# A transformer block with experts on one core: sums of squares on TensorE, lower parts on GpSimd, attention scores a step later

## The chip, the core and the metric

The kernel runs on one core of a Trainium2 chip. The metric is device time in microseconds. Five engines run their own instruction streams, each in the order in which the program wrote them: TensorE (PE), VectorE (DVE), ScalarE (ACT), GpSimd (POOL) and SyncE (SP), which here only issues transfers.

## The reference

One block on 256 tokens and 256 context tokens of width 2048, in fp32. The parts that the change touches:

```python
mod = silu(c) @ ada_w + ada_b              # the same for the context
h   = rmsnorm(x, norm1_g) * (1 + sc1) + sh1    # and hc for the context
# differential attention, 8 heads, keys from context and tokens
s = einsum(q, k) * scale; p = softmax(s); a = p[0] - lam * p[1]
# gated linear attention, 4 heads, in both directions
q_in, k_in, k_st = q * exp(b), k * exp(-b), k * exp(b_last - b)
att = tril(q_in @ k_in.T)
# experts: top 16 of 128 * 128 for each of 8 heads
act = gelu(einsum("pd,ped->pe", h, u[idx])); out = einsum("pe,ped->pd", act * g, v[idx])
```

`rmsnorm(x, g)` is `x * rsqrt(mean(x * x) + eps) * g`.

## The kernel before

Every weight matrix comes through a `Stream` (line 37) in blocks of 128x1024 fp32, 512 KB each. SP loads a block; ScalarE rounds it to a high part (L90); VectorE or GpSimd subtracts to get the low part (L92); TensorE multiplies both. A stream has a few raw buffers, whose next load waits until the parts have been made. Blocks named in `whole` are not split: TensorE takes them as plain fp32 (L339). Which engine makes the low part, `share` says.

Work beside the products is written as generators in `Jobs` lanes: after each step of a product loop `tick` resumes each lane's first job, and a `yield n` puts the next piece n ticks further. Since every engine keeps the written order, the place of a `yield` fixes where the instructions stand between the matmuls.

**First stage** (lines 219 to 358). 64 blocks of the modulation weights, in eight column groups of eight blocks, go through stream `A`; in the last three groups (5, 6 and 7 of 0 to 7) TensorE also makes products of the stage that follows (`pre`, L214 to L216), which need H, the normalized and modulated x, in a high and a low part. `norm_job` loads x, squares it on ScalarE (L295), adds the squares on GpSimd (L296), sums them over the partitions with one matmul (L298), takes the reciprocal root on ScalarE with a Newton step on VectorE (L181 to L183), and multiplies x by it on GpSimd (L303). `cols_job` turns a group's results into columns (L255, L259), and from the second group on every other group starts an `h_job`, which scales and shifts four of x's 16 slices (VectorE, L275), rounds them (ScalarE, L278) and subtracts (VectorE, L281).

**Attention** (`da_head`, L436 and after). Keys and queries `tq` are normalized and rotated on VectorE (last operation L453), `scores(0)` multiplies them (L465), then come maxima, exponentials, the combination of the two softmaxes, and the transposes `turn` (L491). A head's steps run beside product loops of 12 matmuls to a step (L413 to L416).

**Linear attention** (`gla_head`). VectorE makes `q_in`, `k_in` (L640) and `k_st` (L643), TensorE multiplies the first two (`inner`, L653) and transposes the third (`turn`, L667).

**Experts.** After the query products the stream `W` goes on with 256 blocks of `u` and 256 of `v` (L1222, L1223 for `u`), while VectorE finds each token's experts (routing, L1037 and after). `W.share` at L1154 gives three of four lower parts to GpSimd from there on.

Of the kernel before, what the change touches and what calls it, by code (L numbers as in the profile page):

```python
# [7 lines left out]
F32 = mybir.dt.float32  # L8
# [3 lines left out]
AF = mybir.ActivationFunctionType  # L12
OP = mybir.AluOpType
# [6 lines left out]
KT = 16  # L20
EPS = 1e-6
FMAX = 3.0e38
NGA = 8
NPRE = 3
# [111 lines left out]
def block_kernel(ctx, tc, a, out):  # L136
    nc = tc.nc
    ctx.enter_context(tc.manual_schedule())
    V, S, G, PE = nc.vector, nc.scalar, nc.gpsimd, nc.tensor
# [23 lines left out]
    W = Stream(nc, wpool, blocks, 3, 3, 2, on_pool)  # L163
# [7 lines left out]
    eps = cst.tile([128, 1], F32)  # L171
# [3 lines left out]
    def rsqrt(pool, v, shape, name, ytag=None, ttag=None):  # L175

        y = pool.tile(shape, F32, name=name + "y", tag=ytag or name + "y", bufs=1)
        t = pool.tile(shape, F32, name=name + "t", tag=ttag or name + "t", bufs=1)
        S.activation(t, v, AF.Ln, bias=eps[:, 0:1])
        S.activation(y, t, AF.Exp, scale=-0.5)  # L180
        V.scalar_tensor_tensor(t, v, EPS, y, op0=OP.add, op1=OP.mult)  # L181
        V.scalar_tensor_tensor(t, t, -0.5, y, op0=OP.mult, op1=OP.mult)
        V.scalar_tensor_tensor(y, t, 1.5, y, op0=OP.add, op1=OP.mult)  # L183
        return y
# [34 lines left out]
    with ExitStack() as st:  # L219
        p0 = st.enter_context(tc.tile_pool(name="p0", bufs=1))  # L220
        some = {i for i in range(64) if i % 8 in (2, 5)}
        late = set(range(8 * (8 - NPRE), 64))
        crow = p0.tile([16, 128], F32, name="crow", tag="sq", bufs=2)
        nc.scalar.dma_start(crow, a["c_row"])
        A = Stream(nc, p0, [a["ada1"][i] for i in range(64)], 5, 4, 3, some & late, some - late)
        A.load_to(5)
        nc.sync.dma_start(P, a["params"])
        nc.sync.dma_start(K0, a["consts0"])
        gs1 = p0.tile([128, KT, 2], F32)
# [17 lines left out]
        ss = sp("ss")  # L247
        acols = sp("acols")[:, 0:64].rearrange("p (a b) -> p a b", b=2)
        rows, normed = {}, [0]
        tot = p0.tile([128, 512], F32)  # L250

        def cols_job(g):
            r = rows.pop(g)
# [12 lines left out]
                jobs.add("h", h_job(k0), 1)  # L266

        def h_job(k0):
            while normed[0] < k0 + 4:
                yield 1  # L270
            for n in range(6):
                if n < 4:
                    k = k0 + n
                    for s, c0 in ((1, 0), (0, 256)):
                        V.tensor_scalar(xs[:, k, c0:c0 + 256], xs[:, k, c0:c0 + 256], gs1[:, k, s:s + 1],  # L275
                                        ada1[:, k, s:s + 1], op0=OP.mult, op1=OP.add)
                if 1 <= n < 5:
                    S.activation(H[:, 0, k0 + n - 1], xs[:, k0 + n - 1], AF.Copy)  # L278
                if n >= 2:
                    k = k0 + n - 2  # L280
                    V.tensor_tensor(H[:, 1, k], xs[:, k], H[:, 0, k].bitcast(F32), OP.subtract)  # L281
                yield 1

        def norm_job():
            for k in range(0, KT, 4):
                nc.sync.dma_start(xs[:, k:k + 4, 0:256], a["ctx_t"][:, k:k + 4])
                nc.sync.dma_start(xs[:, k:k + 4, 256:512], a["x_t"][:, k:k + 4])
                yield 1
            yield 2
            for k in range(KT):  # L290
                if k == 0:
                    S.activation(tot, xs[:, 0], AF.Square)
                else:
                    sq = p0.tile([128, 512], F32, name="sq", bufs=2)
                    S.activation(sq, xs[:, k], AF.Square)  # L295
                    G.tensor_tensor(tot, tot, sq, OP.add)  # L296
                yield 1
            PE.matmul(ss, o2048, tot, start=True, stop=True)  # L298
            yield 1
            rstd = rsqrt(p0, ss, [128, 512], "n1")  # L300
            yield 2
            for k in range(0, KT, 2):
                G.tensor_tensor(xs[:, k:k + 2], xs[:, k:k + 2],  # L303
                                rstd[:, None, :].to_broadcast([128, 2, 512]), OP.mult)
                normed[0] = k + 2
                yield 1

        def lam_job():
            lamv = p0.tile([128, 4, 64], F32, name="lamv", tag="sq", bufs=2)
# [116 lines left out]
    def da_head(pool, j, tq, sq, sk, vals):  # L426
# [24 lines left out]
        yield 1  # L451
        V.tensor_tensor(xq, xq, K[:, C_COS:C_COS + 256][:, None, :].to_broadcast([128, 2, 256]), OP.mult)
        V.tensor_tensor(xq, xq, sw, OP.add)  # L453
        yield 2
        mx = pool.tile([128, 4], F32, name="mx", bufs=2)
        z = pool.tile([128, 4], F32, name="z", bufs=2)
        r = pool.tile([128, 4], F32, name="r", bufs=2)
# [135 lines left out]
    def gla_head(pool, h, kt, qt, vn, gr):  # L593
# [43 lines left out]
        def state_exp(d):  # L637
            S.activation(ks[d], ks[d], AF.Exp, scale=1.0 / 16)
            V.tensor_tensor(qi[d], qi[d], qt, OP.mult)
            V.tensor_tensor(ki[d], ki[d], kt[:, 256:512], OP.mult)  # L640
# [7 lines left out]
        def inner(d):  # L648
            if d == 0:
                att[0] = sp("att").rearrange("p (d b i) -> p d b i", d=2, b=2)  # L650
            for b in range(2):
                c = slice(b * 128, (b + 1) * 128)
                PE.matmul(att[0][:, d, b], ki[d][:, c], qi[d][:, c], start=True, stop=True)  # L653
# [62 lines left out]
        state_exp(0)  # L716
        yield 1
        decays(1)
        inner(0)
        yield 1  # L720
        state_in(0)
        state_exp(1)
        yield 1
        turn(0)
        inner(1)
        yield 1
        turn_copy(0)
        state_in(1)
        inner_mask()
        yield 1  # L730
        turn(1)
        state_mm(0, 0)
        yield 1
        turn_copy(1)
        state_up(0, 0, 2)
# [192 lines left out]
    with tc.tile_pool(name="xpool", bufs=1) as pool:  # L928
# [7 lines left out]
        sq = {}  # L936
# [214 lines left out]
        if h == 1:  # L1151
            jobs.add("score", rows())
    nwq[0] = W.i
    W.share = lambda s: s % 4 != 0  # L1154
    W.flush()
    jobs.limit("score", 0)
    jobs.add("route", weigh())
# [323 lines left out]
```

## Time and profile before

| what | value |
|---|---|
| median of three runs | 2553.24 us (2549.06 to 2555.9) |
| the profiled execution | 2551.56 us beside a span of 2549.8 |
| TensorE matmuls busy | 2427.0 us, 95% |
| VectorE busy | 1950.9 us, 77% |
| ScalarE busy | 1298.1 us, 51% |
| GpSimd busy | 690.7 us, 27% |
| bytes moved | 678.86 MB, mean 266 GB/s |

Times are in microseconds from the start of the span. Matmuls are pipelined, so the distance between two starts is what one costs in a row; the duration that a row gives is longer. A busy share over the span is an average over stages with different limits.

### The profile page before, as it was taken

The page shows a single profiled execution, that of the slowest core. Times are in us where ns is not written, and L with a number is a line of the kernel's source. Part 1 is how long each engine was busy: PE and PEld are TensorE (multiplying, and loading weights), DVE is VectorE, ACT ScalarE, POOL GpSimd, SP SyncE. Part 2 cuts the span into 40 slices and gives each one's busy share as a digit, 9 for nine tenths or more (in the row PEclk, how much of TensorE's full clock was granted, in tenths as well). Part 3 has the DMA queues.
Part 4 walks back from the last instruction along what each step waited for, and adds up shares of the span by engine and source line. Part 5 has one row for each costly group of instructions (what it writes and reads, how often), then busy time and mean ns, then how long its engine had stood idle before and what let it go on. Part 6 is the DMA issues. An engine that isn't in the chain of part 4 may idle for free.

```text
span 2549.8 us, 39628 instructions
## 1 busy us (share of the span) xinstructions
PE 2427.0 (95%) x15236; PEld 2188.9 (86%) x15236; DVE 1950.9 (77%) x2584; ACT 1298.1 (51%) x1947; POOL 690.7 (27%) x343
## 2 busy tenths in 40 slices
PE   6799999999999999989899999999999999999999
PEld 3477888888899999989898999999998888888887
DVE  4868888657864656457997888889986888888866
ACT  5453444333444444453355999955554444444443
POOL 4441111222201334037487121211120232223100
PEclk8799999999999999999899999999999999999999
DMA  8665555456646776657476899999997999999985
GB/s 299 227 215 185 182 198 173 140 176 247 223 133 206 252 260 217 221 158 236 140 229 217 326 326 325 328 367 393 394 386 263 368 378 384 362 375 380 350 254 159
DMA packets 196494, 678.86 MB, mean 266 GB/s; under 512 B 21840, under 2 KB 54192, under 8 KB 179152
## 3 DMA queue, kind: packets, MB, share of 16 engines
q1 hardware_dynamic: 155456, 521.36, 59.1%
q0 software_dynamic: 19008, 137.44, 13.9%
q10 hardware_dynamic: 21840, 17.53, 2.3%
q8 instruction: 119, 1.95, 0.3%
q14 instruction: 71, 0.58, 0.1%
HBM read 660.83 MB, written 11.68 MB: 264 GB/s over the span
## 4 chain that ended last, share of the span: by engine, by line
PE 66%; DVE 16%; DMA 7%; issue 2%; ACT 2%; ACTq 0%; SPq 0%; POOL 0%; DVEq 0%; POOLq 0%
PE acc L1222 10%; PE acc L214 6%; PE acc L216 6%; PE acc L215 6%; PE yb L1364 5%; PE acc L1223 5%; PE yb L1363 5%; PE ya L1366 4%; PE ya L1367 4%; PE ya L1365 4%; DMA back<-park 4%; DVE wlo L92 2%; PE acc L413 2%; PE acc L415 2%; PE acc L416 2%
## 5 line engine op out<-in xcount | busy, mean ns | idle before, releaser
L92 DVE TENSOR_TENSOR wlo<-wraw,whi 128x1024 fp32r<-128x1024 f32 x669 | 841.2, 1278 | 283.9 <-ACT whi L90 280.0
L90 ACT ACTIVATE whi<-wraw 128x1024 fp32r<-128x1024 f32 x824 | 853.2, 1053 | 277.9 <-PE ya L1366 53.8
L92 POOL TENSOR_TENSOR wlo<-wraw,whi 128x1024 fp32r<-128x1024 f32 x155 | 400.7, 2594 | 786.3 <-ACT whi L90 768.3
L1222 PE MATMUL acc<-H,whi 128*128 128x384 f32 x2048 | 612.0, 364 | 0.0
L1223 PE MATMUL acc<-H,wlo 128*128 128x192 f32 x2048 | 521.6, 255 | 21.3 <-DVE wlo L92 20.9
L1223 PEld LDWEIGHTS acc<-H,wlo 128*128 128x128 f32 x2048 | 394.7, 193 | 27.9 <-DVE wlo L92 27.6
L1222 PEld LDWEIGHTS acc<-H,whi 128*128 128x128 f32 x2048 | 388.7, 190 | 0.0
L214 PE MATMUL acc<-H,whi 128*128 128x256 f32 (+1 forms) x1248 | 377.2, 302 | 1.4 <-ACT whi L90 1.4
L216 PE MATMUL acc<-H,wlo 128*128 128x256 f32 (+1 forms) x1248 | 371.7, 298 | 1.0 <-DVE wlo L92 0.8
L215 PE MATMUL acc<-H,whi 128*128 128x256 f32 (+1 forms) x1248 | 371.3, 298 | 0.0
L214 PEld LDWEIGHTS acc<-H,whi 128*128 128x128 f32 x1248 | 239.2, 192 | 20.3 <-issue 12.1
L216 PEld LDWEIGHTS acc<-H,wlo 128*128 128x128 f32 x1248 | 239.1, 192 | 8.4 <-DVE wlo L92 1.2
L215 PEld LDWEIGHTS acc<-H,whi 128*128 128x128 f32 x1248 | 239.3, 192 | 5.8
L1166 POOL DMA_INDIRECT gat<-v_rows,sidx x64 | 121.0, 1890 | 368.7 <-DVE ys L1188 307.1
L389 DVE SCALAR_TENSOR_TENSOR a<-a,cb 128x1024 f32<-128x1024 f32 x128 | 194.1, 1520 | 23.4 <-DMA a<-ada 23.3
L1363 PE MATMUL yb<-whi,as 128*128 128x512 f32 x512 | 204.2, 399 | 2.6 <-DVE as L191 2.6
L1166 POOL DMA_INDIRECT gat<-u_rows,sidx x64 | 94.3, 1474 | 409.4 <-DVE gat L1173 409.0
L1364 PE MATMUL yb<-wlo,as 128*128 128x512 f32 x512 | 203.9, 398 | 0.4 <-DVE wlo L92 0.4
L1366 PE MATMUL ya<-whi,as 128*128 128x512 f32 x512 | 203.1, 397 | 0.0
L1367 PE MATMUL ya<-wlo,as 128*128 128x512 f32 x512 | 202.7, 396 | 0.0
L1365 PE MATMUL ya<-whi,as 128*128 128x512 f32 x512 | 202.6, 396 | 0.0
L1188 DVE SCALAR_TENSOR_TENSOR ys<-gat,sg,ys 128x2048 f32<-128x2048 f32 x63 | 147.9, 2348 | 24.7 <-DMA gat<-v_rows,sidx 24.7
(327 smaller groups left out, 4156.4 us busy)
## 6 DMA issues: line engine op xcount, KB each, us to landing
wraw<-u SPq DMA_DIRECT2D x256, 512.0 KB
wraw<-v_rows SPq DMA_DIRECT2D x256, 512.0 KB
wraw<-w_a SPq DMA_DIRECT2D x162, 512.0 KB
a<-ada SPq DMA_DIRECT2D x128, 512.0 KB
wraw<-ada SPq DMA_DIRECT2D x64, 512.0 KB
wraw<-w_br SPq DMA_DIRECT2D x32, 512.0 KB
wraw<-w_o SPq DMA_DIRECT2D x32, 512.0 KB
wraw<-w_q SPq DMA_DIRECT2D x32, 512.0 KB
```

Of the source, the lines that this page charges most:

```text
L90: nc.scalar.activation(hi, r, AF.Copy)
L92: e.tensor_tensor(lo, r, hi.bitcast(F32), OP.subtract)
L214: PE.matmul(acc[:, :n], hi[:, c], mh, start=(k == 0), stop=False)
L215: PE.matmul(acc[:, :n], hi[:, c], ml, start=False, stop=False)
L216: PE.matmul(acc[:, :n], lo[:, c], mh, start=False, stop=(k == nk - 1))
L1222: PE.matmul(acc[:, 0:2 * TD], hi[:, c], H2[:, k], start=(k == 0), stop=(k == KT - 1), skip_group_check=True)
L1223: PE.matmul(acc[:, 0:TD], lo[:, c], H2[:, k, 0:TD], start=False, stop=(k == KT - 1), skip_group_check=True)
L1363: PE.matmul(yb[n], hb, hi[:, c], start=first, stop=False)
L1364: PE.matmul(yb[n], hb, lo[:, c], start=False, stop=last)
L1365: PE.matmul(ya[n], h0, hi[:, c], start=first, stop=False)
L1366: PE.matmul(ya[n], h1, hi[:, c], start=False, stop=False)
L1367: PE.matmul(ya[n], h0, lo[:, c], start=False, stop=last)
```

## The change

In the first stage the stream gets six raw buffers instead of five and other blocks for GpSimd and for the unsplit way (in both versions VectorE makes 48 of the 64 lower parts; GpSimd made 6 and makes 10; 10 blocks were unsplit and 6 are). `norm_job` sums the squares with 16 matmuls into one PSUM bank and no longer multiplies x; `h_job` does that, with operations that take two tensors and a scalar. The scores in `da_head` are written one tick later, the two `inner` calls and the mask in `gla_head` one step later. `W.share` gives GpSimd all lower parts of the first twelve expert blocks.

```diff
--- before.py
+++ after.py
@@ -219,11 +219,10 @@
     with ExitStack() as st:
         p0 = st.enter_context(tc.tile_pool(name="p0", bufs=1))
         some = {i for i in range(64) if i % 8 in (2, 5)}
-        late = set(range(8 * (8 - NPRE), 64))
         crow = p0.tile([16, 128], F32, name="crow", tag="sq", bufs=2)
         nc.scalar.dma_start(crow, a["c_row"])
-        A = Stream(nc, p0, [a["ada1"][i] for i in range(64)], 5, 4, 3, some & late, some - late)
-        A.load_to(5)
+        A = Stream(nc, p0, [a["ada1"][i] for i in range(64)], 6, 4, 3, some, {2, 13, 26, 37, 50, 61})
+        A.load_to(6)
         nc.sync.dma_start(P, a["params"])
         nc.sync.dma_start(K0, a["consts0"])
         gs1 = p0.tile([128, KT, 2], F32)
@@ -247,7 +246,7 @@
         ss = sp("ss")
         acols = sp("acols")[:, 0:64].rearrange("p (a b) -> p a b", b=2)
         rows, normed = {}, [0]
-        tot = p0.tile([128, 512], F32)
+        rstd = p0.tile([128, 512], F32)
 
         def cols_job(g):
             r = rows.pop(g)
@@ -266,19 +265,22 @@
                 jobs.add("h", h_job(k0), 1)
 
         def h_job(k0):
-            while normed[0] < k0 + 4:
+            while not normed[0]:
                 yield 1
             for n in range(6):
-                if n < 4:
-                    k = k0 + n
-                    for s, c0 in ((1, 0), (0, 256)):
-                        V.tensor_scalar(xs[:, k, c0:c0 + 256], xs[:, k, c0:c0 + 256], gs1[:, k, s:s + 1],
-                                        ada1[:, k, s:s + 1], op0=OP.mult, op1=OP.add)
-                if 1 <= n < 5:
-                    S.activation(H[:, 0, k0 + n - 1], xs[:, k0 + n - 1], AF.Copy)
-                if n >= 2:
-                    k = k0 + n - 2
-                    V.tensor_tensor(H[:, 1, k], xs[:, k], H[:, 0, k].bitcast(F32), OP.subtract)
+                for c, c0 in ((1, 0), (0, 256)):
+                    t = slice(c0, c0 + 256)
+                    if n < 4:
+                        k = k0 + n
+                        V.scalar_tensor_tensor(xs[:, k, t], xs[:, k, t], gs1[:, k, c:c + 1], rstd[:, t],
+                                               op0=OP.mult, op1=OP.mult)
+                    if 1 <= n < 5:
+                        k = k0 + n - 1
+                        S.activation(H[:, 0, k, t], xs[:, k, t], AF.Identity, bias=ada1[:, k, c:c + 1])
+                    if n >= 2:
+                        k = k0 + n - 2
+                        V.scalar_tensor_tensor(H[:, 1, k, t], xs[:, k, t], ada1[:, k, c:c + 1],
+                                               H[:, 0, k, t].bitcast(F32), op0=OP.add, op1=OP.subtract)
                 yield 1
 
         def norm_job():
@@ -288,22 +290,19 @@
                 yield 1
             yield 2
             for k in range(KT):
-                if k == 0:
-                    S.activation(tot, xs[:, 0], AF.Square)
-                else:
-                    sq = p0.tile([128, 512], F32, name="sq", bufs=2)
-                    S.activation(sq, xs[:, k], AF.Square)
-                    G.tensor_tensor(tot, tot, sq, OP.add)
+                sq = p0.tile([128, 512], F32, name="sq", bufs=2)
+                S.activation(sq, xs[:, k], AF.Square)
                 yield 1
-            PE.matmul(ss, o2048, tot, start=True, stop=True)
+                PE.matmul(ss, o2048, sq, start=(k == 0), stop=(k == KT - 1))
             yield 1
-            rstd = rsqrt(p0, ss, [128, 512], "n1")
-            yield 2
-            for k in range(0, KT, 2):
-                G.tensor_tensor(xs[:, k:k + 2], xs[:, k:k + 2],
-                                rstd[:, None, :].to_broadcast([128, 2, 512]), OP.mult)
-                normed[0] = k + 2
-                yield 1
+            t = p0.tile([128, 512], F32, name="sq", bufs=2)
+            S.activation(t, ss, AF.Ln, bias=eps[:, 0:1])
+            S.activation(rstd, t, AF.Exp, scale=-0.5)
+            V.scalar_tensor_tensor(t, ss, EPS, rstd, op0=OP.add, op1=OP.mult)
+            V.scalar_tensor_tensor(t, t, -0.5, rstd, op0=OP.mult, op1=OP.mult)
+            V.scalar_tensor_tensor(rstd, t, 1.5, rstd, op0=OP.add, op1=OP.mult)
+            normed[0] = 1
+            yield 1
 
         def lam_job():
             lamv = p0.tile([128, 4, 64], F32, name="lamv", tag="sq", bufs=2)
@@ -451,7 +450,7 @@
         yield 1
         V.tensor_tensor(xq, xq, K[:, C_COS:C_COS + 256][:, None, :].to_broadcast([128, 2, 256]), OP.mult)
         V.tensor_tensor(xq, xq, sw, OP.add)
-        yield 2
+        yield 3
         mx = pool.tile([128, 4], F32, name="mx", bufs=2)
         z = pool.tile([128, 4], F32, name="z", bufs=2)
         r = pool.tile([128, 4], F32, name="r", bufs=2)
@@ -716,20 +715,20 @@
         state_exp(0)
         yield 1
         decays(1)
-        inner(0)
         yield 1
         state_in(0)
         state_exp(1)
+        inner(0)
         yield 1
         turn(0)
-        inner(1)
         yield 1
         turn_copy(0)
         state_in(1)
-        inner_mask()
+        inner(1)
         yield 1
         turn(1)
         state_mm(0, 0)
+        inner_mask()
         yield 1
         turn_copy(1)
         state_up(0, 0, 2)
@@ -1151,7 +1150,7 @@
         if h == 1:
             jobs.add("score", rows())
     nwq[0] = W.i
-    W.share = lambda s: s % 4 != 0
+    W.share = lambda s: s % 4 != 0 or s < nwq[0] + 12
     W.flush()
     jobs.limit("score", 0)
     jobs.add("route", weigh())
```

Three places in the engines' order show what moves. First VectorE, from the Newton step on (before L181 to L183, after L301 to L303); `wlo` is a lower part, `H` the low part of the normalized x. Before:

```order
L181 SCALAR_TENSOR_TENSOR n1t<-sp,n1y 128x512
L182 SCALAR_TENSOR_TENSOR n1t<-n1t,n1y 128x512
L183 SCALAR_TENSOR_TENSOR n1y<-n1t,n1y 128x512
L92 TENSOR_TENSOR wlo<-wraw,whi 128x1024
L259 TENSOR_TENSOR ada_102<-sp,P 128x8
L92 TENSOR_TENSOR wlo<-wraw,whi 128x1024
L275 TENSOR_SCALAR xs<-xs,gs_101,ada_102 128x256 x4
L92 TENSOR_TENSOR wlo<-wraw,whi 128x1024
L275 TENSOR_SCALAR xs<-xs,gs_101,ada_102 128x256 x2
L281 TENSOR_TENSOR H<-xs,H 128x512
L92 TENSOR_TENSOR wlo<-wraw,whi 128x1024
L275 TENSOR_SCALAR xs<-xs,gs_101,ada_102 128x256 x2
```

After:

```order
L301 SCALAR_TENSOR_TENSOR sq<-sp,rstd 128x512
L302 SCALAR_TENSOR_TENSOR sq<-sq,rstd 128x512
L303 SCALAR_TENSOR_TENSOR rstd<-sq,rstd 128x512
L275 SCALAR_TENSOR_TENSOR xs<-xs,gs_103,rstd 128x256 x4
L92 TENSOR_TENSOR wlo<-wraw,whi 128x1024
L258 TENSOR_TENSOR ada_104<-sp,P 128x8
L275 SCALAR_TENSOR_TENSOR xs<-xs,gs_103,rstd 128x256
L282 SCALAR_TENSOR_TENSOR H<-xs,ada_104,H 128x256
L275 SCALAR_TENSOR_TENSOR xs<-xs,gs_103,rstd 128x256
L282 SCALAR_TENSOR_TENSOR H<-xs,ada_104,H 128x256
L92 TENSOR_TENSOR wlo<-wraw,whi 128x1024
```

The scaling now has `rstd` as its second tensor, the subtraction comes in halves, and the first four scalings stand ahead of the lower part that came right after Newton's step.

Second TensorE in the linear attention, around the transposes (before L667, after L666) and the inner products (before L653, after L652); the other rows are the product loop. Before:

```order
L415 MATMUL acc<-wlo,H 128x256
L416 MATMUL acc<-whi,H 128x256
L667 MATMUL sp<-K_67,k_st 128x128 x4
L653 MATMUL sp<-q_in,k_in 128x128 x2
L413 MATMUL acc<-whi,H 128x256
```

After:

```order
L414 MATMUL acc<-wlo,H 128x256
L415 MATMUL acc<-whi,H 128x256
L666 MATMUL sp<-K_67,k_st 128x128 x4
L412 MATMUL acc<-whi,H 128x256
L414 MATMUL acc<-wlo,H 128x256
```

The inner product no longer follows the transposes at once: in the new order it stands at the end of the step after them, 12 matmuls on.

```order
L414 MATMUL acc<-wlo,H 128x256
L415 MATMUL acc<-whi,H 128x256
L652 MATMUL sp<-q_in,k_in 128x128 x2
L412 MATMUL acc<-whi,H 128x256
L414 MATMUL acc<-wlo,H 128x256
```

Third VectorE in the routing beside the first expert blocks, around a lower part that GpSimd now makes. Before:

```order
L1040 MAX top<-cand 128x8
L1041 MAX_INDEX pos<-top,cand 128x8
L92 TENSOR_TENSOR wlo<-wraw,whi 128x1024
L1075 TENSOR_SCALAR pu<-pos 128x16
L1076 TENSOR_SCALAR pu<-pos 128x16
L1079 TENSOR_TENSOR oh<-pu,iota 128x512
```

After:

```order
L1039 MAX top<-cand 128x8
L1040 MAX_INDEX pos<-top,cand 128x8
L1074 TENSOR_SCALAR pu<-pos 128x16
L1075 TENSOR_SCALAR pu<-pos 128x16
L1078 TENSOR_TENSOR oh<-pu,iota 128x512
```

Three such rows are gone in all (the other two stand within 28 rows behind it); GpSimd's run of lower parts at this place has 66 instead of 63.

## Rows read from the trace of the kernel before

**Rows 1.** The page, part 4: the chain of work that ended last, shares of the span by engine.
```profile
PE 66%; DVE 16%; DMA 7%; issue 2%; ACT 2%; ACTq 0%; SPq 0%; POOL 0%; DVEq 0%; POOLq 0%
```

**Rows 2.** TensorE's waits over the whole span, grouped by the waiting line and by what it waited for: us in total, how many, the longest.
```profile
PE acc L1223 <- DVE wlo L92: 20.9, 16, 5.9
PE acc L342 <- DVE wlo L92: 16.0, 10, 5.5
PE sp L465 <- DVE tq L453: 15.5, 8, 3.9
...
PE sp L653 <- DVE k_in L640: 10.9, 4, 3.5
...
PE sp L491 <- DVE pt L486: 0.9, 1, 0.9
```

**Rows 3.** Four stretches of the first stage: length, busy us and instructions of PE, PEld, DVE, ACT and POOL, the granted TensorE clock, the busy share of the DMA engines, GB/s.
```profile
0.00:64.00 64.00, 42.95 (x111) 19.74 (x111) 31.00 (x27) 33.69 (x43) 31.00 (x22) 0.81 0.86 299
64.00:98.00 34.00, 20.43 (x59) 11.57 (x58) 32.21 (x27) 12.58 (x16) 21.69 (x8) 0.66 0.46 154
98.00:116.00 18.00, 14.99 (x44) 7.84 (x43) 15.25 (x26) 10.88 (x14) 5.06 (x2) 0.78 0.88 319
116.00:163.00 47.00, 44.95 (x182) 35.55 (x180) 31.10 (x30) 25.57 (x29) 18.97 (x7) 0.90 0.72 237
```

**Rows 4.** GpSimd's timeline in the first stage: start, us, engine, line, operation, output and inputs, shapes, number, idle time before and what ended it. L296 adds squares, L303 multiplies x by the reciprocal root.
```profile
36.52 26.66 POOL L296 TENSOR_TENSOR tot<-tot,sq 128x512 f32<-128x512 f32 x13 [5.44 <-ACT sq L295]
68.00 21.69 POOL L303 TENSOR_TENSOR xs<-xs,n1y 128x1024 f32<-128x1024 f32 x8 [4.82 <-DVE n1y L183]
```

**Rows 5.** TensorE's timeline in the first stage, same columns: two unsplit blocks (L339, four records each are two fp32 matmuls of 512 columns), matmuls of split blocks (L341 with the high part, L342 with the low), the longest stall.
```profile
40.97 3.32 PE L339 MATMUL acc<-wraw,cf 128*4 128x512 f32 x4
...
69.77 1.88 PE L339 MATMUL acc<-wraw,cf 128*4 128x512 f32 x4
...
71.91 0.39 PE L342 MATMUL acc<-wlo,cm 128*128 128x512 f32 x1
72.14 0.40 PE L341 MATMUL acc<-whi,cm 128*128 128x512 f32 x1
...
85.17 0.80 PE L342 MATMUL acc<-wlo,cm 128*128 128x512 f32 x1 [5.54 <-DVE wlo L92]
```

**Rows 6.** VectorE's timeline in the same stretch: Newton's step (L183), lower parts of weight blocks (L92), the scaling of x (L275).
```profile
67.23 0.69 DVE L183 SCALAR_TENSOR_TENSOR n1y<-n1t,n1y 128x512 f32<-128x512 f32 x1
...
69.05 3.32 DVE L92 TENSOR_TENSOR wlo<-wraw,whi 128x1024 fp32r<-128x1024 f32 x1
72.29 9.52 DVE L275 TENSOR_SCALAR xs<-xs,gs,ada 128x256 f32<-128x256 f32 x4
...
90.36 1.21 DVE L92 TENSOR_TENSOR wlo<-wraw,whi 128x1024 fp32r<-128x1024 f32 x1
...
97.97 0.73 DVE L275 TENSOR_SCALAR xs<-xs,gs,ada 128x256 f32<-128x256 f32 x2
```

**Rows 7.** VectorE's timeline in the attention stage: an operation of two tensors and a scalar on 128x256.
```profile
234.46 0.43 DVE L547 SCALAR_TENSOR_TENSOR ot<-ot,oy 128x256 f32<-128x256 f32 x1
```

**Rows 8.** TensorE's timeline in the attention stage: scores (L465) that wait for tq, and matmuls of the product loop (L415) one step of 12 apart.
```profile
242.87 2.08 PE L465 MATMUL sp<-tq 64*128 64x512 f32 x4 [3.73 <-DVE tq L453]
...
281.63 1.13 PE L465 MATMUL sp<-tq 64*128 64x512 f32 x4 [1.18 <-DVE tq L453]
...
282.91 0.28 PE L415 MATMUL acc<-wlo,H 128*128 128x256 f32 x1
...
284.34 0.28 PE L415 MATMUL acc<-wlo,H 128*128 128x256 f32 x1
...
318.30 1.13 PE L465 MATMUL sp<-tq 64*128 64x512 f32 x4 [1.87 <-DVE tq L453]
...
466.64 1.62 PE L465 MATMUL sp<-tq 64*128 64x512 f32 x4 [3.92 <-DVE tq L453]
```

**Rows 9.** VectorE's timeline in the linear attention: the multiplication that completes k_st of direction 0, in two of the four heads.
```profile
537.77 0.68 DVE L643 TENSOR_TENSOR k_st<-k_st,kt 128x512 f32<-128x512 f32 x1
...
608.55 0.68 DVE L643 TENSOR_TENSOR k_st<-k_st,kt 128x512 f32<-128x512 f32 x1
```

**Rows 10.** TensorE's timeline in the same heads: the transposes of k_st (turn(0), L667).
```profile
538.89 0.60 PE L667 MATMUL sp<-K,k_st 128*128 128x128 f32 x4
...
610.74 0.60 PE L667 MATMUL sp<-K,k_st 128*128 128x128 f32 x4
```

**Rows 11.** VectorE's timeline at the first expert blocks: lower parts.
```profile
1264.93 1.21 DVE L92 TENSOR_TENSOR wlo<-wraw,whi 128x1024 fp32r<-128x1024 f32 x1
...
1282.43 2.52 DVE L92 TENSOR_TENSOR wlo<-wraw,whi 128x1024 fp32r<-128x1024 f32 x1
```

**Rows 12.** TensorE's timeline there: the first product of an expert block with a lower part.
```profile
1254.57 0.53 PE L1223 MATMUL acc<-H,wlo 128*128 128x192 f32 x1 [5.92 <-DVE wlo L92]
...
1266.19 0.53 PE L1223 MATMUL acc<-H,wlo 128*128 128x192 f32 x1 [4.71 <-DVE wlo L92]
```

**Rows 13.** GpSimd's timeline there: the lower part before that of 1264.93.
```profile
1262.66 2.35 POOL L92 TENSOR_TENSOR wlo<-wraw,whi 128x1024 fp32r<-128x1024 f32 x1 [0.45 <-ACT whi L90]
```

**Rows 14.** The stretch of the first expert blocks up to the next standstill of TensorE, columns as in rows 3.
```profile
1266.00:1358.00 92.00, 88.51 (x594) 87.74 (x594) 86.61 (x193) 47.06 (x72) 68.84 (x27) 0.96 0.71 226
```

## The prediction

> **What bounds the kernel now.** I read the page first. The chain that ended last is two thirds TensorE, with VectorE far behind it [rows 1]: most of the program is TensorE work in a row, and what a change elsewhere is worth is read from the places where TensorE stands. The sums of its waits name four such places that the diff touches [rows 2]: the products of the first stage (L342), the scores (L465), the inner products of the linear attention (L653) and the first expert products (L1223). Then the first stage was cut at the ends of its column groups [rows 3]. Until 64 us the transfers are busy for 0.86 of the time at 299 GB/s; from 64 to 98 TensorE is busy for 20.4 of 34 us at a granted clock of 0.66, VectorE for 32.2 and GpSimd for 21.7: there VectorE binds and TensorE waits. From 98 to 116 VectorE is still busy for 15.25 of 18 us; from 116 to 163 TensorE binds with 44.95 of 47.
>
> Why VectorE binds: GpSimd's adds pace the sum of squares from 36.5 to 63.2 and its eight multiplies run from 68.0 to 89.7 [rows 4], and beside the multiplies VectorE's scaling of one 128x256 piece takes 2.4 us (9.52 for four) against 0.36 later, and a lower part 3.3 us against 1.21 [rows 6]. TensorE's stall of 5.54 us before 85.17 is the result [rows 5].
>
> **The sum of squares.** Removed: 15 GpSimd adds and one sum on TensorE. Added: 16 sums, each with its 512 columns in unsplit fp32. A block that goes through TensorE unsplit is two such matmuls (four records in the trace); it takes 1.88 us at 2.4 GHz and 3.32 at 1.2 GHz [rows 5], so one sum is 0.9 or 1.7 us. From 36.5 us on some twelve split blocks of 0.92 us (four matmuls 0.23 apart, 71.91 to 72.14), twelve sums of 0.9, one unsplit block and the columns of a group come to 24.5 us, where the adds took 26.7. I take −2; bounds −6 (no clock dip) and +13 (half of these columns at 1.2 GHz).
>
> **From the sum to the end of group 3 (column groups counted 0 to 7).** The last sum now ends at 64 − 2, and Newton's three operations end 2 us after the activations, about as before; call the start 64. What VectorE does before it can write the columns of group 3, which it did just ahead of 97.97 [rows 6], at 97.5: Newton 3 × 0.69 = 2.1; the first h job, 16 operations on 128x256. Two tensors and a scalar make one operation; such a one takes 0.43 us elsewhere [rows 7], 0.46 with its spacing: 7.2. Seven lower parts at 1.21: 8.5. One part on GpSimd in this group, which lengthens a VectorE operation by 1.3 (2.52 against 1.21, [rows 11]). Hand-overs to ScalarE, which now adds the bias and rounds: 3, an estimate of about 0.2 for each operation that waits for one. 64 + 22.1 = 86 against 97.5: **−11.5, of which −9.5 is new**. Bounds: −18 (TensorE would bind next) and 0 (each operation as stretched as beside the multiplies).
>
> The skill speaks against this step. The rows first: the removed scaling is 0.365 a piece once GpSimd rests (0.73 for two, [rows 6]), the new one 0.43 to 0.46 [rows 7]. The Trainium skill (VectorE: DVE Perf Modes, Mode 2×_2P) says that an fp32 operation on one tensor and a scalar uses both read ports and gets two results a cycle, and one on two tensors cannot; by its 0.96 GHz the scaling of a 256-column piece would lose 0.13 us, my estimate, or 1.1 us a group, where the rows make it 0.8. Trace and page agree in sign, and the loss lies inside the 7.2. The second rule is on GpSimd. By rows, a part on GpSimd of 2.35 us lengthens one VectorE operation by 1.3. The Trainium skill (GPSIMD Engine Reference, 8. Key points) says that GpSimd contends with VectorE operations that have two SBUF inputs, which all the new ones are; were each held for the whole part, the two parts of groups 3 and 4 would cost 2 us more in all than I charge.
>
> **The rest of the stage.** Group 4: six lower parts 7.3, the h job 7.2, one GpSimd part 1.3, small ones and hand-overs 1.4: 17.2 against the 18 of [rows 3], −0.8. Groups 5 to 7 are bound by TensorE; two of the unsplit blocks now lie there, each 0.96 us dearer than a split one: +1.9. The last h job, −1, and one clock dip less after a stall, −1. **Stage: −2 − 9.5 − 0.8 + 1.9 − 2 = −12**, bounds −26 and +3. The transfers allow it: the first 116 us move 64 us at 299 GB/s, 34 at 154 and 18 at 319, 30.1 MB [rows 3], which at 299 GB/s are there by 101 us, and I have group 4 end at 104.
>
> **Attention.** The step before the scores is doubled from two ticks to three. TensorE waits eight times for tq, 15.5 us, twice for over 3.7 and six times for 7.85 in all [rows 2, 8]. A step of 12 matmuls is 1.43 us (282.91 to 284.34, [rows 8]). Each wait loses at most one step: 7.4 of the short ones (one is longer than a step) and 2 × 1.43 of the long: **−10.3**. A head is 20 ticks instead of 19, two heads 40, and the unit has 40, so nothing is pushed out of it. Bounds: −13 (clock dips after the long waits go too) and −4 (VectorE, asked sooner for the next work, gives part back at the turns).
>
> **Linear attention.** The inner products come a step later, so the four waits of 10.9 us at L653 lose most of their length, but turn(0), one step behind, needs k_st, and VectorE ends that only 0.44 to 1.5 us before TensorE now asks for it [rows 9, 10] (537.77 + 0.68 to 538.89; 608.55 + 0.68 to 610.74). Four times about 1.1 is a cap of 4.4. I take **−3.5**; bounds 0 and −8.
>
> **Experts.** The rule names twelve blocks, but nine were GpSimd's already and the first two were split before the rule is set: three lower parts change hands, those of 1264.93, 1282.43 [rows 11] and one between. The first wait (5.92) stays, the second (4.71 before 1266.19, [rows 12]) should go: GpSimd's part before it began at 1262.66 and took 2.35 [rows 13]. GpSimd at 2.35 a part keeps TensorE's pace: 88.5 us for 594 matmuls, 16 a block, is 2.4 a block [rows 14]. But VectorE, with the routing, is busy for 86.6 of the 92 us to 1358 [rows 14], where TensorE waits next; the gain cannot exceed the 1.21 + 1.21 + 2.52 taken from it and what was idle, some 6.7. I take **−6**; bounds −2 and −10.
>
> **Sum:** −12 − 10.3 − 3.5 − 6 = −31.8. The profiled execution took 2551.6 us; the median of the three runs is 1.7 above it, inside their spread of 6.8, and is left out. 2551.6 − 31.8 = **2520 us**. All that follows is TensorE in a row and only moves forward. A difference below 0.3%, 7.7 us, counts as no change.
>
> **Rivals.**
> A. The first stage loses its standstill altogether, and transfers or TensorE bind it. For it: VectorE's 32 us in the second window is stretched work. Against: even unstretched, its work there is 22 us. The stage would give −25: 2507. Chance 0.13.
> B. VectorE binds and the waits move on: the scores come later but the turns and the outputs wait for the same VectorE, which is late because of its queue and not because of TensorE's order. One wait of 0.9 us at a turn (L491) was there before [rows 2]. Attention returns nothing, linear attention nothing, stage −12, experts −4: 2535.5. Chance 0.2.
> C. Slower: the 16 sums hold TensorE at 1.2 GHz. Before, half clock stood in the rows after standstills (the unsplit block at 40.97 took 3.32, those from 69.77 1.88). A sum then costs 1.7, a block 1.7, sixteen of both end at 91 instead of 64; VectorE's gain takes 9.5 of the 27 off, and if group 5 is at 1.2 GHz too, it takes 17 us more. With +1.9 and the other three terms, −19.8: +15, 2566. It decides whether half clock outlasts group 4; if not, the whole is no change. Chance 0.06, and 0.04 for no change by this way.
> D. The change does less than it says: for the experts it does, as told (three blocks, not twelve), and the sum is made with three.
>
> **How the numbers follow.** Forecast 0.57 (2508 to 2532 by its bounds), A 0.13, B 0.2, C 0.06 slower and 0.04 same. Some of B's bounds reach no change: 0.04. So faster 0.86, same 0.08, slower 0.06. The range runs from below A, 2499, to above B, 2541.
>
> **What would show it.** In the profile after, GpSimd has no L296 or L303; the last sum of squares ends between 58 and 66 us; the second window's end comes near 86 and group 5 begins near 104 with a clock over 0.8; waits at L464 (the scores) sum to 5 us or less with none of equal size new at L490 (the turns); those at L652 and L666 sum to about 7; the expert wait near 1266 is gone. The prediction is wrong if the clock stays at 0.5 from 36 to 100 us, if VectorE's new operations take a microsecond each, or if waits of the old size stand one step further on.

## The result, and the profile after

The changed kernel takes 2579.05 us (median of nine runs, 2570.35 to 2582.43) where the kernel before takes 2555.9 in nine runs beside it: the ratio is 1.0087, interval [1.007, 1.0104], slower by some 22 us where 32 fewer were forecast. The profiled execution has 2579.05 us, its span 2577.2.

The first question is where. The same instructions can be found in both traces, and the difference of their starts tells how far the changed kernel is ahead (−) or behind (+):

| TensorE reaches | before, us | after − before, us |
|---|---|---|
| columns of group 3 | 95.6 | −13.7 |
| columns of group 7, end of the first stage | 162.6 | −10.9 |
| scores of head 3 | 281.6 | −9.8 |
| scores of head 5 | 354.5 | +2.6 |
| scores of head 8 | 466.6 | +15.7 |
| linear attention, first to last transposes | 538.9 to 750.9 | +14.1 to +15.7 |
| sum of squares of the second normalization | 1125.2 | +16.9 |
| last transposes of hsum, beside the query products | 1180.9 | +25.4 |
| expert products, 3% done | 1282.4 | +20.2 |
| expert products, a quarter done | 1429.3 | +29.3 |
| last matmul | 2543.9 | +26.9 |

The first stage won what was forecast, the attention lost 25 us, the query products 8 to 9, the experts won 7 and gave 9 back. The stage's windows, which answer to [rows 3], same columns:

```profile
0.00:64.00 64.00, 52.00 (x160) 30.77 (x160) 28.98 (x31) 39.39 (x50) 11.73 (x11) 0.92 0.92 328
64.00:98.00 34.00, 25.41 (x67) 13.53 (x66) 31.00 (x51) 24.57 (x36) 9.05 (x4) 0.73 0.75 248
98.00:116.00 18.00, 18.00 (x63) 14.34 (x64) 12.48 (x10) 7.57 (x9) 6.93 (x3) 0.74 0.83 265
116.00:163.00 47.00, 42.11 (x158) 29.37 (x157) 34.93 (x46) 24.19 (x35) 13.29 (x5) 0.89 0.46 151
```

TensorE's clock from 64 to 98 us is 0.73 instead of 0.66, GpSimd is out of VectorE's way, and from 98 to 116 TensorE is busy throughout, at a clock of 0.74 instead of 0.78. The last sum of squares starts at 59.0 us in TensorE's timeline:

```profile
59.00 1.02 PE L296 MATMUL sp<-sq,o 128*128 128x512 f32 x2
```

VectorE's timeline in the same stage answers to [rows 6]: the new scaling (L275), the subtraction in halves (L282), the columns of groups 3 and 4 (L258):

```profile
63.62 1.67 DVE L275 SCALAR_TENSOR_TENSOR xs<-xs,gs,rstd 128x256 f32<-128x256 f32 x4
...
67.64 0.48 DVE L282 SCALAR_TENSOR_TENSOR H<-xs,ada,H 128x256 fp32r<-128x256 f32 x1
...
70.36 2.59 DVE L282 SCALAR_TENSOR_TENSOR H<-xs,ada,H 128x256 fp32r<-128x256 f32 x1
...
85.11 0.15 DVE L258 TENSOR_TENSOR ada<-sp,P 128x8 f32<-128x8 f32 x1
...
102.94 0.15 DVE L258 TENSOR_TENSOR ada<-sp,P 128x8 f32<-128x8 f32 x1
```

Four scalings take 1.67 us instead of 9.52; the columns of group 3 are written at 85.1 and those of group 4 at 102.9, where the prediction had 86 and 104. One subtraction takes 2.59 us instead of 0.48; it stands beside a lower part that GpSimd makes from 70.08 us on, in 2.58 us.

TensorE's waits over the whole span, the answer to [rows 2], show the loss as a scattering of small ones:

```profile
PE acc L1222 <- DVE wlo L92: 24.0, 19, 7.8
PE sp L464 <- DVE tq L452: 12.7, 7, 3.5
PE acc L341 <- DVE wlo L92: 9.3, 9, 2.0
PE sp L666 <- DVE k_st L642: 6.6, 3, 2.4
...
PE hrow L1130 <- DVE hsum L1127: 6.5, 1, 6.5
PE sp L527 <- DVE al L516: 5.6, 2, 2.8
...
PE sp L490 <- DVE pt L485: 4.7, 6, 2.2
...
PE sp L652 <- DVE k_in L639: 4.1, 2, 2.1
...
PE acc L414 <- POOL wlo L92: 3.5, 2, 2.0
```

The scores still wait (12.7 us, L464), the turns wait for more than before (L490, 4.7 us instead of 0.9), and there are waits at the output products (L527) and at weight blocks from GpSimd (L414) that were not there before. None says why. The reason is on the queues of ScalarE and VectorE at the start of a head. ScalarE's timeline in the changed kernel, where head 4 starts (its first matmul is at 299.79 us) and head 3 is put out (`ot`, `oy`, `YA`):

```profile
300.85 0.69 ACT L438 ACTIVATE rkt<-sp,eps 128x512 f32<-128x512 f32 x1 [1.49 <-PE sp L427]
...
302.39 0.21 ACT L439 ACTIVATE rq<-rqt 128x4 f32<-128x4 f32 x1
302.50 0.46 ACT L541 ACTIVATE ot<-sp,eps 128x256 f32<-128x256 f32 x1
302.99 0.42 ACT L542 ACTIVATE oy<-ot 128x256 f32<-128x256 f32 x1
309.08 0.42 ACT L550 ACTIVATE YA<-og 128x256 fp32r<-128x256 f32 x1 [5.68 <-DVE og L548]
309.41 1.99 ACT L90 ACTIVATE whi<-wraw 128x1024 fp32r<-128x1024 f32 x2
```

And in the kernel before at the same place (head 4 starts at 305.41):

```profile
304.43 0.48 ACT L542 ACTIVATE ot<-sp,eps 128x256 f32<-128x256 f32 x1
304.94 0.42 ACT L543 ACTIVATE oy<-ot 128x256 f32<-128x256 f32 x1
306.47 0.69 ACT L439 ACTIVATE rkt<-sp,eps 128x512 f32<-128x512 f32 x1 [1.11 <-PE sp L428]
...
308.00 0.20 ACT L440 ACTIVATE rq<-rqt 128x4 f32<-128x4 f32 x1
308.12 0.40 ACT L551 ACTIVATE YA<-og 128x256 fp32r<-128x256 f32 x1
308.42 1.05 ACT L90 ACTIVATE whi<-wraw 128x1024 fp32r<-128x1024 f32 x1
```

Before, the output's logarithm and exponential (`ot`, `oy`) stand ahead of the head's four activations, and the high part of the next weight block (L90) starts 3.0 us after the head. In the changed kernel they stand behind the four, ScalarE then waits 5.68 us for `og` with two weight blocks behind it, and the first of them starts 9.6 us after the head. What `og` waits for is in VectorE's timeline:

```profile
302.99 0.42 DVE L543 TENSOR_SCALAR ov<-sp 128x256 f32<-128x256 f32 x1 [3.95 <-ACT ot L541]
...
304.47 0.69 DVE L421 SCALAR_TENSOR_TENSOR rkt<-sp,rk 128x512 f32<-128x512 f32 x1
...
306.64 0.69 DVE L442 TENSOR_TENSOR tq<-tq,rk 128x512 f32<-128x512 f32 x1
307.25 0.42 DVE L545 TENSOR_TENSOR ot<-ov,oy 128x256 f32<-128x256 f32 x1
...
308.63 0.42 DVE L548 TENSOR_TENSOR og<-og,oy 128x256 f32<-128x256 f32 x1
...
311.03 2.58 DVE L552 TENSOR_TENSOR YA<-og,YA 128x256 fp32r<-128x256 f32 x1
...
315.40 0.69 DVE L452 TENSOR_TENSOR tq<-tq,sw 128x512 f32<-128x512 f32 x1
```

VectorE stands 3.95 us at `ov`, which it gets only when `ot` has left ScalarE; then the head's Newton step and scaling of tq are ahead of the output's four operations, which end at 309.05. The output's last operation (`YA`, L552) comes ahead of the end of tq as well, and beside a part on GpSimd (2.80 us from 310.53) it takes 2.58 us, where it took 0.42 before. tq itself is complete at 316.1, 16.3 us after the head's start; before, it took 12.7. TensorE pays at both ends:

```profile
313.39 0.50 PE L216 MATMUL acc<-H,wlo 128*128 128x512 f32 x1 [1.70 <-POOL wlo L92]
...
316.24 2.08 PE L464 MATMUL sp<-tq 64*128 64x512 f32 x4 [1.65 <-DVE tq L452]
```

A late block (1.70) and late scores (1.65), after which four matmuls of the scores take 2.08 us instead of 1.13 ([rows 8] have both): the clock has dropped. From 190 to 500 us the granted clock is 0.94, before 0.98. TensorE's waits in that stretch are 28.2 us instead of 16.4, which is 12 of the 25 us lost; 0.04 of 310 us is another 12, an estimate of what the lower clock costs.

### The profile page after: what moved, and what is told of

It reads as the page before. It is cut to its first block, busy times and chain, and to the rows that moved or that the text cites. A ratio compares the mean times of both kernels' runs of the same rounds, so it can differ in the third digit from the quotient of the medians.

```text
span 2577.2 us, 39682 instructions
## 1 busy us (share of the span) xinstructions
PE 2447.7 (95%) x15266; PEld 2205.5 (86%) x15266; DVE 1942.0 (75%) x2597; ACT 1303.8 (51%) x1967; POOL 664.1 (26%) x327
## 3 DMA queue, kind: packets, MB, share of 16 engines
q0 software_dynamic: 19008, 137.44, 13.7%
## 4 chain that ended last, share of the span: by engine, by line
PE 70%; DVE 18%; DMA 6%; ACT 3%; issue 2%; ACTq 0%; POOL 0%; SPq 0%; DVEq 0%; POOLq 0%
PE acc L1221 10%; PE acc L214 6%; PE acc L216 6%; PE acc L215 6%; PE yb L1362 5%; PE ya L1366 5%; PE yb L1363 5%; PE ya L1365 5%; PE ya L1364 5%; PE acc L1222 4%; DMA back<-park 3%; DVE wlo L92 3%; DVE a L388 2%; PE sp L1280 2%; PE acc L412 2%
## 5 line engine op out<-in xcount | busy, mean ns | idle before, releaser
L92 DVE TENSOR_TENSOR wlo<-wraw,whi 128x1024 fp32r<-128x1024 f32 x666 | 830.4, 1268 | 302.8 <-ACT whi L90 296.9
L90 ACT ACTIVATE whi<-wraw 128x1024 fp32r<-128x1024 f32 x828 | 855.0, 1052 | 253.8 <-PE ya L1365 57.4
L92 POOL TENSOR_TENSOR wlo<-wraw,whi 128x1024 fp32r<-128x1024 f32 x162 | 418.8, 2595 | 882.0 <-ACT whi L90 785.9
L1165 POOL DMA_INDIRECT gat<-v_rows,sidx x64 | 127.8, 1997 | 360.8 <-DVE ys L1187 301.1
L388 DVE SCALAR_TENSOR_TENSOR a<-a,cb 128x1024 f32<-128x1024 f32 x128 | 183.9, 1441 | 25.9 <-DMA a<-ada 25.7
```

Of the source, the lines that this page charges most:

```text
L90: nc.scalar.activation(hi, r, AF.Copy)
L92: e.tensor_tensor(lo, r, hi.bitcast(F32), OP.subtract)
```

## The experiments

Theory C, from these rows: the head now ends a tick later, the output job `da_out`, which is started by that end, moves with it and falls on the tick on which the next head starts. Rivals: T, later scores only hand their waits on to the turns; E, another part of the change moves the attention. Four kernels tell them apart.

**a_noscore**: the changed kernel without the step.

```diff
-        yield 3
+        yield 2
```

> The changed kernel with the wait before scores(0) back at two ticks; all else of the change stays. Theory C (a head now ends one tick later, so that the output job's normalization falls on the tick on which the next head starts) and theory T (later scores only hand their waits to the turns and output products) both say that the loss of about 25 us in the attention goes: 2579 - 25 = 2554, or down to 2545. Theory E (another part of the change shifts the attention): stays at 2575 to 2582. In the trace the scores of the eighth head stand at 456 (C, T) or 482 (E).

2552.49 us, 0.9993 of before [0.998, 1.0006]. Its scores of head 8 stand at 456.0, −10.6. E falls: the loss is that of the step. That it is not faster than before is taken up under b_stage.

**b_score**: the step alone, in the kernel before.

```diff
-        yield 2
+        yield 3
```

> The kernel before with the scores one tick later and nothing else. C and T: slower by 20 to 27 us, 2576 to 2583; ScalarE's waits for og at YA rise from 4.5 us to over 30. E: within 5 us of before, or faster by up to the 10 us that the prediction had.

2578.38 us, 1.0089 [1.0069, 1.0109]: the whole loss of the change. TensorE's waits in the attention are those of the changed kernel, to 0.1 us: 12.7 at the scores, 5.6 at the output products, 4.7 at the turns, 3.5 and 1.8 at weight blocks from GpSimd. Together they are 28 us instead of the 16.4 that the kernel before has in the same stretch, in five places instead of two.

**b_collide**: the scores stay, the output job starts a tick later.

```diff
-        jobs.add("db", da_out(pool, j, ah, al, vals["h"], vals["l"]), 1)
+        jobs.add("db", da_out(pool, j, ah, al, vals["h"], vals["l"]), 2)
```

> The kernel before with the output job of a head started one tick later (it waits two ticks instead of one); the scores stay where they were. By the written order its sum of squares stands right behind the next head's first matmuls, as in the changed kernel. C: slower by 15 to 27 us, with ScalarE's waits at YA over 25 us. T and E: within 4 us of before.

2582.59 us, 1.0115 [1.0088, 1.0141]. The scores are where they were, and the loss is there: theory C. TensorE's and ScalarE's waits in the attention:

```profile
PE sp L465 <- DVE tq L453: 29.3, 7, 7.1
```

```profile
ACT YA L551 <- DVE og L549: 35.9, 7, 5.7
```

With the scores in their old place the lateness of tq shows undivided: 29.3 us instead of 15.5 in this stretch, and TensorE waits for nothing else there. The step of b_score took back part of it and met other waits instead. (The profiled execution is the shortest of the four, 2570.91 us.)

**b_score_same_end**: scores a tick later, the end of the head kept.

```diff
-        yield 2
+        yield 3
...
         scores(0)
-        yield 2
+        yield 1
         maxima(0)
```

> The kernel before with the scores one tick later and the maxima at their old tick (one tick behind the scores instead of two), so that the head's end and the output job stay where they were. C: no loss; between 2545 and 2558, and the waits at the scores sum to about 5 us. T: slower by 10 to 25 us, with waits at the turns.

2555.92 us, 1.0004 [0.9988, 1.0021]: no loss, as C says. No gain either, and here T has a share: the waits at the scores fall to 5.0 us, those at the turns and output products rise to 9.4.

```profile
PE sp L491 <- DVE pt L486: 5.4, 3, 2.2
PE sp L465 <- DVE tq L453: 5.0, 3, 2.5
PE sp L528 <- DVE al L517: 4.0, 3, 2.8
```

Next, what in the collision costs, and whether the prediction's gain is there without it.

**b_dbfirst**: the output job on the same tick as in b_collide, but written ahead of the head (its lane is ticked first).

```diff
+    jobs.lanes["db"], jobs.lanes["da"] = [], []
```

> As b_collide (the kernel before, output job on the same tick as the next head's start), but with the output job written ahead of the head on that tick, so that on ScalarE its two activations stand before the head's four, and on VectorE its four operations before the head's Newton step. If it is the order on the two queues that costs (the output's chain waits behind the head's on ScalarE, and the next weight block behind YA), the loss goes: 2550 to 2560 and under 10 us of ScalarE's waits at YA. If it is the amount of work on one tick, the loss stays: 2570 to 2585.

2563.07 us, 1.0027 [1.0013, 1.0042]. Same work on the same tick in the other order: 20 of the 28 us are gone. The rest, 7, stays with the work on one tick also in this order; no third order was tried. The result lies between the two ranges of the expectation, which had the order or the amount of work, not both. ScalarE's waits at YA and TensorE's at the scores:

```profile
ACT YA L551 <- DVE og L549: 4.3, 7, 1.2
```

```profile
PE sp L465 <- DVE tq L453: 17.1, 8, 4.1
```

**b_db6**: the output job six ticks later instead of one.

```diff
-        jobs.add("db", da_out(pool, j, ah, al, vals["h"], vals["l"]), 1)
+        jobs.add("db", da_out(pool, j, ah, al, vals["h"], vals["l"]), 6)
```

> The kernel before with the output job six ticks later, past the head's first bursts on VectorE; the scores as they were. Theory C: nothing collides, within 8 us of before, faster by up to 8 if the normalization of the last head was part of what the scores wait for (their 15.5 us). If any later output costs, slower by 10 us or more.

2548.86 us, 0.997 [0.9956, 0.9984]. Part of what the scores waited for was the last head's normalization ahead of tq on VectorE: their wait is 0.9 us instead of 15.5. More than half of that comes back at the turns, which waited 0.9 us before:

```profile
PE sp L491 <- DVE pt L486: 9.8, 6, 2.2
```

In this kernel ScalarE waits 28 us at YA, and the kernel is faster, so that such a wait is a mark of the collision and not its price. A weight block stands behind six of these seven waits, too, so that block alone is not the price either; what TensorE waited for in b_collide was tq.

**b_score_db6**: both.

> The kernel before with the scores one tick later and the output job six ticks later. Theory C: the loss of 24 us goes, and the term of the prediction shows: waits at the scores of 5 us instead of 15.5, 2543 to 2550. Theory T (later scores hand their waits on): waits at the turns and at the output products instead, 2553 to 2560.

2544.35 us, 0.9956 [0.9942, 0.997]: 11 us faster, of which 7 come from moving the output job; the 4 that are left for the step are hardly clear of the noise, since the two intervals overlap. TensorE's waits in the attention:

```profile
PE sp L491 <- DVE pt L486: 7.5, 5, 2.2
PE sp L465 <- DVE tq L453: 0.2, 1, 0.2
```

The scores wait for nothing; the turns wait for 7.5 us. C was right and T took a share.

Then the other parts alone.

**b_stage**: the first stage alone (all of the diff up to `lam_job`).

> The kernel before with the first stage of the change alone. By the landmarks of the changed kernel the stage ends 10 to 12 us earlier. Theory K (the gain is kept, since what follows is TensorE in a row): 2543, 0.9957 of before. Theory G (the stretch of the query products gives it back, as in the changed kernel with the scores at two ticks): 2550 to 2555, with a wait of 6 us at the first transposes of hsum that the kernel before shows in some executions only.

2550.12 us, 0.9982 [0.9968, 0.9995]. The starts, set against the kernel before as in the table, are −15.6 us at the end of the stage, −13.0 through the attention, −10.1 at 1125, −6.2 at 1181 (with a wait of 2.9 us for hsum), −2.5 at the end. The stage's gain is real and two thirds of it are not in the median; G (given back) is nearer than K (kept). Where it goes is told below.

**b_gla**: the linear attention alone.

> The kernel before with the inner products and their mask one step later and nothing else. The prediction's own term: -3.5 us. The rival that the wait goes on to the transposes (turn) one step behind: 0 to +2, with waits at L667 of 6 to 8 us in all and some 4 left at L653.

2555.57 us, 1.0011 [1.0001, 1.0022]. TensorE's waits there:

```profile
PE sp L667 <- DVE k_st L643: 5.8, 3, 2.4
PE sp L653 <- DVE k_in L640: 3.8, 2, 2.0
```

9.6 us instead of 10.9 (11.3 and 1.0 in the second profile of the kernel before), with most of it now at the transposes: the rival. It gains nothing, and may cost 0.1%.

**b_share**: the expert blocks alone.

> The kernel before with the three lower parts at the first expert blocks given to GpSimd and nothing else. The prediction's own term: -6 us. The rival that VectorE, which the routing keeps busy, is late at the first part that is its own again: the wait of 4.7 us near 1266 goes, a wait of 3 to 6 us comes near 1295 to 1320, and the sum is within 2 us of before.

2550.96 us, 0.9992 [0.9978, 1.0006]. The rival again:

```profile
1257.43 0.53 PE L1223 MATMUL acc<-H,wlo 128*128 128x192 f32 x1 [7.79 <-DVE wlo L92]
...
1298.03 0.53 PE L1223 MATMUL acc<-H,wlo 128*128 128x192 f32 x1 [5.83 <-DVE wlo L92]
```

The wait that [rows 12] show at 1266 is gone, and one of 5.83 us stands at the fifteenth block, the first lower part that VectorE makes itself again, behind its routing. VectorE starts that part at 1296.77, before at 1292.90: later, although three parts were taken from it on the way. The reason is beside it. GpSimd is busy for 31.9 us between the part of the second block and this one, before for 20.0, and VectorE's routing operations there add up to 35.6 us instead of 28.0. The first `oh` on that way in the kernel before, and the same operation in b_share, where GpSimd makes two parts in the 4.77 us from 1267.76 on:

```profile
1266.33 0.69 DVE L1079 TENSOR_TENSOR oh<-pu,iota 128x512 f32<-128x512 uint32 x1
```

```profile
1270.31 2.77 DVE L1079 TENSOR_TENSOR oh<-pu,iota 128x512 f32<-128x512 uint32 x1
```

The first wait grows for the same reason, 7.79 us instead of 5.92: `cand` (L1068), ahead of that block's lower part, takes 2.30 us instead of 0.41 beside the first of two parts of GpSimd. All three kernels with the new share have it (7.79 to 7.80), the eleven others do not (5.90 to 5.93).

**before_again** was the kernel before, for a second profile of the query products.

> The kernel before once more, for a second profile of the query products. If the wait at the first transposes of hsum belongs to the execution and not to the change, it is 0 in some profiles of unchanged code and 6 to 7 us in others; if it is a consequence of the change, it is 0 here again.

2552.43 us, no wait for hsum. So there is none in both profiles of the kernel before, nor in those of b_collide and b_dbfirst, and between 1.1 and 7.2 us in those of the ten other kernels, whose code is the same at this place. What goes with the wait is the length of the two routing operations `oh` that VectorE has ahead of hsum. The second of them, in the kernel before, where GpSimd's next part starts at 1167.76, and in the changed one, where GpSimd makes parts without a break from 1183.81 to 1197.44:

```profile
1167.63 0.69 DVE L1082 TENSOR_TENSOR oh<-oh,iu 128x512 f32<-128x512 f32 x1
```

```profile
1189.17 2.78 DVE L1081 TENSOR_TENSOR oh<-oh,iu 128x512 f32<-128x512 f32 x1
```

Where both take 0.69 us, the wait is 0 to 2.3; where one takes 2.76 (b_stage, stage_score_db6), 2.9; where both take 2.77 or 2.78 (the changed kernel, a_noscore, b_score_same_end), 6.2 to 7.2. At the expert blocks this second profile has waits of 16.6 us at L1223 up to 1420 us, the same as b_share in three waits (7.79, 5.83, 3.00); and between 1294 and 1324 us it loses 5 us against the first profile, so that the differences in that stretch are not all the change's.

**stage_score_db6**: the version that these runs point to: the first stage of the change, the scores a tick later, the output job six ticks later.

> The first stage of the change, the scores one tick later and the output job six ticks later; linear attention and expert blocks as before. If the gains of b_stage (5 us) and of b_score_db6 add: 2538 to 2546, faster than both kernels. If theory T holds for the scores: as b_stage, 2550.

2540.25 us, 0.9944 [0.9925, 0.9964]: 14 us faster than the kernel before (9 to 19 by the interval) and 39 faster than the changed one. Added, the gains of b_stage and b_score_db6 are 16: the result agrees with that, but the interval also reaches the 11 of b_score_db6 alone.

## Why the prediction was wrong

**The step that failed** is one sentence on the attention: "A head is 20 ticks instead of 19, two heads 40, and the unit has 40, so nothing is pushed out of it." It counted the ticks of the head's own lane. A job that the head starts at its end lies in another lane and moves too, onto the tick on which the next head starts, and there ScalarE's and VectorE's written order puts it behind the head's work. The changed order was there to be read: in it the output's sum (L536) stands right behind the next head's first matmuls (L427), where before, from the third head on, it stood 7 or 13 rows ahead of them. The trace before even had one case of it: at the second head that sum (L537, 228.92 us) stands behind the head's start (L428, 227.70), ScalarE waits 4.53 us at YA, and the scores of 242.87 [rows 8] wait 3.73 us. Forecast −10.3, measured +25. Nor was the gain there without the collision: with the head's end kept by a tick less ahead of the maxima (b_score_same_end) the step took the scores' waits to 5.0 us and won nothing, because 9.4 us stood at the turns and the output products. Rival B had the mechanism next to it (the waits move on, nothing is won) and not this one, so its 2535 was too low as well; rival C did not come about, since the granted clock up to 98 us rose (0.92 and 0.73 instead of 0.81 and 0.66). Its own terms add up to +16.6, not +15.

**The first stage** came out as worked out: the last sum ended at 60 (62 forecast), group 3 at 85.1 (86), group 4 at 102.9 (104), −10.9 at the end of the stage (−12; −15.6 in b_stage, whose code is the same there). The new scaling's 0.42 to 0.48 us are near the 0.43 of [rows 7]. One charge was too small: a part on GpSimd lengthens a two-tensor operation by 2.1 us (2.59 against 0.48), not by the 1.3 that I charged; [rows 6] had it, with 3.32 against 1.21. The Trainium skill (GPSIMD Engine Reference, 8. Key points) says that GpSimd contends with VectorE operations that have two SBUF inputs. The trace agrees: the 2.1 us are most of the 2.58 of GpSimd's part.

**What follows is not TensorE in a row that only moves forward.** That sentence of the sum was wrong too: of the 13 us that b_stage has in hand at the end of the attention, 2.5 are left in its profile and 5 in the ratio. In the profile 3 go between the attention and 1125 us, 4 at the query products, where TensorE waits for hsum and VectorE's routing is lengthened beside lower parts on GpSimd (before_again), and 4 in the expert blocks and later. What lets those parts fall on the routing in one kernel and not in another is not settled; it was not separated whether it is the time of arrival or how the transfers of that stretch fall.

**Linear attention:** forecast −3.5, measured +2.8 (0.3 to 5.6 by the interval). The cap by k_st was named, and the wait went there nearly in full. **Experts:** forecast −6, measured −2 (−5.6 to +1.5 by the interval of b_share). In the changed kernel TensorE is 7 us nearer to the kernel before from 1259 to 1282 us and loses them again, and in b_share the waits of the stretch sum to what before_again has. The bound was written down, that VectorE is busy for 86.6 of 92 us, and still the full gain was booked. The step that failed here is the sum of what is taken from VectorE: it took 5 us of lower parts away and put at nothing what more parts on GpSimd do to VectorE's other work, which grew by 7.7 us in b_share (35.6 against 28.0).

## What to carry to other kernels

Where jobs are written in lanes that are ticked together, a delay of one step moves all that is started by its end: look in the written order of each engine for what it now stands beside, above all two chains that cross the same two engines. Of two such chains on one tick, write the one first that is further along, or move one of them off that tick (b_db6). And a wait that is taken from an engine with little idle time in that stretch is looked for again at that engine's next piece of work, before it is booked. Work that goes from VectorE to GpSimd is priced with what it adds to the VectorE operations that will then stand beside it.

## What the runs showed that was not expected

The order of the same work on one tick was worth 20 us (b_collide 2582.59, b_dbfirst 2563.07). A wait of ScalarE of 28 us in all can cost nothing (b_db6) or stand beside a loss of 24 us (b_score, 36.0 us). Behind it stands one weight block in the first kernel and mostly two in the second; whether that makes the difference was not tried. Three lower parts given to GpSimd left VectorE with more work and not less. And a stretch with unchanged code waited between 0 and 7.2 us for the same operation in profiles of different kernels, along with the length of two VectorE operations ahead of it.
